# A small store in a two-layer hybrid trunk: the final n of the mLSTM leaves from a 128x4 tile of its own instead of from a column of a larger tile

## The chip, the core and the metric

One core of a Trainium2 chip runs the whole program in one launch. The metric is the device time in microseconds (us), the median of several runs. Names used below: PE is TensorE, with its weight loads beside it; DVE is VectorE; ACT is ScalarE; POOL is GpSimd; SP is SyncE, which here issues almost all DMAs. HBM is the chip's main memory, SBUF the core's own.

## The reference, cut to what matters

Two decoder layers run on 256 prompt positions and 8 single-token samples, 264 columns together. In each layer one input projection feeds three groups of heads (sliding-window attention, a Mamba-2 scan, an mLSTM); an output projection and a squared-ReLU MLP follow. The outputs are the two hidden states and every final state. The part that matters here is the mLSTM over the prompt, in two chunks of 128 positions, for 4 heads of 128 dimensions:

```
C = C * g_end[..., None, None] + einsum('bhk,bkhd,bkhe->bhde', wk, kc, vc)
n = n * g_end[..., None]       + einsum('bhk,bkhd->bhd', wk, kc)
return ..., C, n, m_new        # final C (4,128,128), final n (4,128), per layer
```

The final n of the prompt is an output called n_p: per layer 128 rows of 4 numbers (one per head), 2 KB in all. The kernel gets n with C in one matmul, since the values carry a column of ones behind their 128 columns; C is then 128 columns wide and n is column 128.

## The kernel before, in words

All weights come from HBM in float32 and are used as two parts. A step loads half a weight block, 128 x 1024 numbers (512 KB), into a tile `raw` (3 buffers). ACT casts it into `hi`, DVE subtracts and leaves the rest in `lo`, and PE runs 24 matmuls of 264 columns on it: `acc<-uh,hi` and `acc<-ul,hi` eight times each, then `acc<-uh,lo` eight times. Two such halves make one output block, and 43 blocks make the input projection of a layer.

The work of the three head groups is laid between these matmuls. Nothing is executed in the order in which the source is written: each operation is recorded first (line 196), and `issue` (line 267) simulates the engines with estimated costs and due times and writes each engine's list. All instructions then come from line 410, so the profile puts them all on that line, and they are told apart by tile names. A DMA gets the same cost whatever the size of its pieces: 0.4 us on its queue and its bytes over a fixed rate (line 248). The lists are fixed. An engine that waits for one instruction holds back all that follow it on that engine. Loads of weights and stores of results share SP's one list, and their transfers share the same DMA engines.

The mLSTM is in `mlstm()` (line 1075). Names that the profile shows there: `lB` is a large buffer, whose part `Co` (line 1083) has 4 heads of 130 columns, C in columns 0 to 127 and n in column 128; `hB` holds the weighted keys and the values; `eA` takes the exponentials and squares of ACT; `mw` is a tile of small numbers per row for the normaliser; `srow` holds rows of q and k for the samples. Lines 1132 and 1133 store C_p (128 rows x 4 heads x 512 bytes) and n_p, each by one DMA on SP. The second reads column 128 of `Co`, whose heads are 130 numbers apart, so each of its 512 pieces is one number of 4 bytes. Behind it lie the loop over the two chunks (line 1138) and the mLSTM of the samples (line 1190).

Of the kernel before, what the change touches and what calls it, by code (L numbers as in the profile page):

```python
# [18 lines left out]
P = 128  # L19
# [409 lines left out]
def trunk(ctx, tc, I, O):  # L429
    nc = tc.nc  # L430
    pr = Program(tc)
    vec, act, pool, pe, sync = pr.vec, pr.act, pr.pool, pr.pe, pr.sync
# [8 lines left out]
    def st(shape, tag, dt=F32, bufs=1):  # L441
        return pr.tile(sp, shape, dt, tag, bufs)
# [118 lines left out]
    def mixers(l):  # L561
# [500 lines left out]
        def m_evac(i):  # L1062
            def f(acc):
                if i == 0:
                    t_["m3"] = st((P, 12, T), "m3")
                dst = t_["m3"][:, i]
                if i < 4:
                    stt(out=dst, in0=acc, scalar=KSC, in1=rb, op0=MUL, op1=MUL)
                else:
                    tt(out=dst, in0=acc, in1=rb, op=MUL)  # L1070
                if i == 11:
                    mlstm()
            return f

        def mlstm():
# [7 lines left out]
            Co = MD[:, 520:1040].rearrange("p (h e) -> p h e", h=4)  # L1083
# [46 lines left out]
                for h in range(2):  # L1130
                    stt(out=Co[:, h0 + h, 0:129], in0=C0[:, h0 + h, 0:129], scalar=EG[:, h0 + h, 151:152], in1=cp_[:, h, 0:129], op0=MUL, op1=ADD)
            sync.dma_start(out=O["C_p"][l], in_=Co[:, :, 0:P])
            sync.dma_start(out=O["n_p"][l], in_=Co[:, :, 128])
            qg = st((P, 4, P), "Qm")
            ptt(out=qg, in0=mq[:, :, P:256], in1=EG[:, :, 24:152], op=MUL)

# [394 lines left out]
```

## Time and profile before

| what | value |
|---|---|
| median of 3 runs | 2375.81 us (2373.26 to 2376.09) |
| the profiled execution's own time | 2372.86 us |
| its span, first to last instruction | 2371.1 us |
| PE busy in the span | 2324.2 us (98%) |
| DVE, ACT, POOL busy | 1483.0, 1173.6, 60.6 us |
| mean granted TensorE clock | 0.994 |
| DMA moved | 432.27 MB, mean 182 GB/s |

The profiled execution took 1.8 us more than its span, for what lies around the instructions. A share of busy time is an average over the program; what a change is worth is read from the few microseconds around it. A timeline row gives start, duration, engine, operation, out<-in by tile names, shape and count, and in brackets the idle time before it with what ended it. SPq is the issuing of a DMA, not its transfer. Rows of one kind that follow each other are merged, so "x4" with a long duration spans the waits between the four.

### The profile page before, as it was taken

What the parts mean: (1) busy time and instruction counts of PE and PEld (TensorE: products, weight loads), DVE (VectorE), ACT (ScalarE), POOL (GpSimd) and SP (SyncE); (2) the same over time, 40 slices, a digit from 0 to 9 for tenths busy, and PEclk for the clock granted to TensorE, in tenths of its full rate; (3) what the DMA queues carried; (4) which work ended last, traced back from release to release, by engine and by line L of the source; (5) the groups of instructions that cost most, each with busy time, mean ns of one, the idle gap of its engine ahead of it and who ended that gap; (6) DMA issues with size and microseconds to landing.
All of it is one profiled execution on the core that took longest, in us unless ns stands there. A gap on an engine that the chain in (4) does not pass through costs nothing.

```text
span 2371.1 us, 46293 instructions
## 1 busy us (share of the span) xinstructions
PE 2324.2 (98%) x18874; PEld 2306.8 (97%) x18874; DVE 1483.0 (63%) x2450; ACT 1173.6 (49%) x1979; POOL 60.6 (3%) x138
## 2 busy tenths in 40 slices
PE   8999799999999999999999999999999999999997
PEld 7999799999999999999999998999999999999997
DVE  8789796754554454455686898866545545544555
ACT  5657564543453344354545577455434434434553
POOL 0120000000000000000001100000000000000000
PEclk9999999999999999999999999999999999999999
DMA  7356666555655565565563577555556556655654
GB/s 249 109 181 219 178 213 180 182 180 180 181 182 179 180 184 179 181 183 179 179 201 120 160 249 215 183 182 181 180 180 183 179 179 183 181 179 182 183 178 135
DMA packets 124052, 432.27 MB, mean 182 GB/s; under 512 B 15808, under 2 KB 19264, under 8 KB 123840
## 3 DMA queue, kind: packets, MB, share of 16 engines
q1 hardware_dynamic: 123264, 428.10, 58.9%
q8 instruction: 149, 2.44, 0.4%
q10 hardware_dynamic: 576, 1.22, 0.1%
q14 instruction: 63, 0.52, 0.1%
HBM read 410.10 MB, written 19.16 MB: 181 GB/s over the span
## 4 chain that ended last, share of the span: by engine, by line
PE 91%; DVE 4%; DMA 3%; ACT 1%; issue 1%; SPq 0%; DVEq 0%; ACTq 0%
PE acc L410 86%; PE ms L410 4%; DMA raw<-in_w_in 2%; DVE lo L410 1%; PE sg L410 1%; DMA S<-in_ssm 1%; DMA out_ssm_s<-S 1%; DVE S L410 0%; DVE ac L410 0%; ACT hi L410 0%; DVE m L410 0%; DVE tb L410 0%; DVE xt L410 0%; SPq L410 0%; ACT eA L410 0%
## 5 line engine op out<-in xcount | busy, mean ns | idle before, releaser
L410 ACT CAST hi<-raw 128x1024 fp32r<-128x1024 f32 (+1 forms) x751 | 783.4, 1044 | 979.4 <-PE acc L410 924.1
L410 DVE TENSOR_TENSOR lo<-raw,hi 128x1024 fp32r<-128x1024 f32 (+1 forms) x751 | 912.0, 1215 | 343.6 <-ACT hi L410 336.8
L410 PE MATMUL acc<-uh,hi 128*128 128x264 f32 x3392 | 856.0, 287 | 11.4 <-ACT hi L410 9.0
L410 PE MATMUL acc<-ul,hi 128*128 128x264 f32 x3392 | 847.9, 285 | 0.0
L410 PEld LDWEIGHTS acc<-uh,hi 128*128 128x128 f32 x3392 | 640.8, 189 | 14.6 <-ACT hi L410 10.6
L410 PEld LDWEIGHTS acc<-ul,hi 128*128 128x128 f32 x3392 | 641.2, 189 | 3.6 <-issue 1.4
L410 PE MATMUL acc<-uh,lo 128*128 128x264 f32 x3392 | 484.9, 285 | 0.0
L410 PEld LDWEIGHTS acc<-uh,lo 128*128 128x128 f32 x3392 | 443.3, 189 | 0.6 <-issue 0.5
L410 PE MATMUL acc<-lB,hi 128*128 128x264 f32 x1280 | 320.4, 286 | 0.0
L410 PE MATMUL acc<-hB,hi 128*128 128x264 f32 x1280 | 320.3, 284 | 0.0
L410 PE MATMUL acc<-hA,hi 128*128 128x264 f32 x1280 | 320.2, 285 | 0.0
L410 PE MATMUL acc<-lA,hi 128*128 128x264 f32 x1280 | 319.4, 285 | 0.0
L410 DVE TENSOR_TENSOR xt<-acc,xt 128x264 f32<-128x264 f32 x192 | 83.0, 432 | 264.0 <-PE acc L410 264.0
L410 PEld LDWEIGHTS acc<-hB,hi 128*128 128x128 f32 x1280 | 241.5, 189 | 0.0
L410 PEld LDWEIGHTS acc<-lB,hi 128*128 128x128 f32 x1280 | 241.3, 189 | 0.0
L410 PEld LDWEIGHTS acc<-hA,hi 128*128 128x128 f32 x1280 | 241.1, 188 | 0.0
L410 PEld LDWEIGHTS acc<-lA,hi 128*128 128x128 f32 x1280 | 241.1, 188 | 0.0
L410 PE MATMUL acc<-hB,lo 128*128 128x264 f32 x1280 | 180.9, 284 | 0.0
L410 PE MATMUL acc<-hA,lo 128*128 128x264 f32 x1280 | 180.6, 284 | 0.0
L410 DVE SCALAR_TENSOR_TENSOR ra<-acc,rb 128x264 f32<-128x264 f32 x128 | 55.4, 432 | 197.0 <-PE acc L410 197.0
L410 PEld LDWEIGHTS acc<-hB,lo 128*128 128x128 f32 x1280 | 165.9, 188 | 0.0
L410 PEld LDWEIGHTS acc<-hA,lo 128*128 128x128 f32 x1280 | 164.4, 188 | 0.0
(305 smaller groups left out, 1374.9 us busy)
## 6 DMA issues: line engine op xcount, KB each, us to landing
raw<-in_w_up SPq DMA_DIRECT2D x256, 512.0 KB, 3.6
raw<-in_w_down SPq DMA_DIRECT2D x256, 512.0 KB, 3.6
raw<-in_w_in SPq DMA_DIRECT2D x171, 512.0 KB, 4.2
raw<-in_w_out SPq DMA_DIRECT2D x64, 512.0 KB, 3.6
S<-in_ssm SPq DMA_DIRECT2D x16, 512.0 KB, 5.4
out_ssm_s<-S SPq DMA_DIRECT2D x16, 512.0 KB, 3.6
S<-in_mC SPq DMA_DIRECT2D x8, 512.0 KB, 5.5
out_C_s<-S SPq DMA_DIRECT2D x8, 512.0 KB, 5.1
```

The source lines that it names most:

```text
L410: getattr(eng, method)(*[real(a) for a in args], **{k: real(a) for k, a in kw.items()})
```

## The change

In each of the two layers, ACT copies column 128 of `Co` (4 numbers per row, 130 apart) into a new tile `np`, 128 rows of 4 numbers side by side. The DMA to n_p then reads this tile: 128 pieces of 16 bytes. No other line differs.

```
-            sync.dma_start(out=O["n_p"][l], in_=Co[:, :, 128])
+            np_out = st((P, 4), "np")
+            act.copy(out=np_out, in_=Co[:, :, 128])
+            sync.dma_start(out=O["n_p"][l], in_=np_out)
```

The lists of PE, DVE and POOL stay the same row by row. ACT's list gains one row in each layer. The piece of ACT's list around it in the first layer, where `eA<-sg,qc` are the four exponentials of the first chunk and the cast `hi<-raw` behind them is that of the next weight half (+ marks what is new):

```order
 L410 CAST hi<-raw 128x1024 x3
 L410 ACTIVATE eA<-sg,qc 128x128 x4
+L410 COPY np<-lB 128x4
 L410 CAST hi<-raw 128x1024
 L410 ACTIVATE eA,mw<-ms 128x128 x4
```

The copy stands between the exponentials and that cast; nothing else moved on ACT. The second place is SP's list around the store of n_p, in the first layer too (the second layer's reads the same, but for the names of buffers):

```order
 L410 DMA out_C_p<-lB 512x1x128
-L410 DMA out_n_p<-lB 512x1x1
-L410 DMA raw<-in_w_in 128x1024 x4
+L410 DMA raw<-in_w_in 128x1024
+L410 DMA out_n_p<-np 128x4
+L410 DMA raw<-in_w_in 128x1024 x3
 L410 DMA n0s<-in_mn 128x32
 L410 DMA raw<-in_w_in 128x1024
```

The store of n_p moved behind the first of the four weight loads that followed it, and it now waits for the copy on ACT.

## Rows read from the trace of the kernel before

**Rows 1.** The page: span, busy time and share of PE and its weight loads.

```profile
span 2371.1 us, 46293 instructions
...
PE 2324.2 (98%) x18874; PEld 2306.8 (97%) x18874; DVE 1483.0 (63%) x2450; ACT 1173.6 (49%) x1979; POOL 60.6 (3%) x138
```

**Rows 2.** PE's waits, whole span: releaser, total us, times, longest us.

```profile
PE sg L410 <- ACT eA L410: 14.6, 2, 10.0
```

**Rows 3.** Timeline of PE, first layer.

```profile
249.47 0.39 PE L410 MATMUL sg<-maskb,identb 128*128 128x512 bf16 x1 [1.87 <-DVE S L410]
...
261.28 1.14 PE L410 MATMUL acc<-uh,lo 128*128 128x264 f32 x8
272.38 0.79 PE L410 MATMUL sg<-srow,ssel 128*128 128x512 f32 x1 [9.95 <-ACT eA L410]
```

**Rows 4.** Timeline of ACT, first layer.

```profile
253.61 1.11 ACT L410 ACTIVATE eA<-sg,qc 128x128 f32<-128x128 f32 x4
267.89 1.04 ACT L410 CAST hi<-raw 128x1024 fp32r<-128x1024 f32 x1 [13.16 <-DMA raw<-in_w_in]
...
271.18 1.15 ACT L410 ACTIVATE eA<-sg,qc 128x128 f32<-128x128 f32 x4
272.17 1.08 ACT L410 CAST hi<-raw 128x1024 fp32r<-128x1024 f32 x1
```

**Rows 5.** Timeline of SP's issues, first layer.

```profile
252.07 1.53 SPq L410 DMA_DIRECT2D out_C_p<-lB  x1
253.65 0.63 SPq L410 DMA_DIRECT2D out_n_p<-lB  x1
254.38 16.16 SPq L410 DMA_DIRECT2D raw<-in_w_in  x4
```

**Rows 6.** Chain that ended last, first layer: start, us, what.

```profile
254.38 13.41 DMA raw<-in_w_in
```

**Rows 7.** Windows: us, busy per engine (instructions), PEclk, DMA share, GB/s.

```profile
250.00:255.00 5.00, 5.00 (x44) 5.00 (x43) 5.00 (x14) 4.72 (x10) 1.26 (x1) 1.00 0.67 254
256.00:265.00 9.00, 6.17 (x50) 5.75 (x49) 2.24 (x5) 0.00 (x0) 1.39 (x2) 1.00 0.57 22
1429.00:1433.00 4.00, 4.00 (x36) 4.00 (x35) 1.83 (x5) 0.00 (x0) 0.67 (x1) 1.00 0.77 42
45.50:48.50 3.00, 3.00 (x27) 3.00 (x27) 2.82 (x6) 1.48 (x2) 0.00 (x0) 1.00 1.03 329
262.40:272.40 10.00, 0.05 (x2) 0.02 (x1) 2.66 (x11) 3.30 (x14) 0.00 (x0) 0.66 0.74 166
272.40:275.80 3.40, 3.40 (x12) 2.86 (x13) 3.19 (x11) 1.28 (x2) 0.00 (x0) 0.50 0.24 88
1439.90:1443.10 3.20, 3.19 (x11) 2.65 (x12) 2.99 (x10) 1.32 (x2) 0.00 (x0) 0.50 0.23 83
```

**Rows 8.** Timeline of SP's issues, first layer: small stores ahead of three loads.

```profile
43.30 0.55 SPq L410 DMA_DIRECT2D out_k_p<-tb  x1
43.90 0.57 SPq L410 DMA_DIRECT2D out_v_new<-vnew  x1
```

**Rows 9.** Tile raw: the three loads issued from 45.8 to 52.0 us.

```profile
DMA to landing us min/median/max: 4.9/5.0/5.1
```

**Rows 10.** Timeline of SP, second layer.

```profile
1425.30 0.67 SPq L410 DMA_DIRECT2D out_n_p<-lB  x1
1426.07 12.01 SPq L410 DMA_DIRECT2D raw<-in_w_in  x4
```

**Rows 11.** Timeline of ACT, second layer.

```profile
1426.21 1.11 ACT L410 ACTIVATE eA<-sg,qc 128x128 f32<-128x128 f32 x4
```

**Rows 12.** Second layer: timeline of PE.

```profile
1439.91 0.80 PE L410 MATMUL sg<-srow,ssel 128*128 128x512 f32 x1 [4.66 <-ACT eA L410]
```

**Rows 13.** Second layer: the chain that ended last.

```profile
1426.07 9.26 DMA raw<-in_w_in
```

**Rows 14.** ACT's groups by form: count, busy us, mean ns, idle before.

```profile
L410 ACT COPY dec<-ms 128x16 f32<-128x16 f32 x2 | 0.3, 172 | 0.1
```

## The prediction

> **What bounds the kernel now.** The page comes first: PE is busy for 98% of the span [rows 1], so only a wait of PE, or a slower PE, can be won back. The list of PE's waits comes next. Its largest entry is one pair: `sg` waits for ACT's `eA`, twice, 14.6 us together, 10.0 the longer [rows 2]. The timelines place the pair: 9.95 us before 272.38 in the first layer [rows 3] and 4.66 us before 1439.91 in the second [rows 12], each soon after the store of n_p.
>
> Going back along the first: PE's `sg<-srow` needs the second four exponentials on ACT, which start at 271.18. They stand in ACT's list behind the cast of one weight half, and that cast began at 267.89 after ACT had stood idle for 13.16 us waiting for the load [rows 4]. So PE waits although its own weights are not what it lacks; a cast ahead in ACT's list is late. The load is the first on SP behind the store of n_p [rows 5], issued at 254.38 and 13.41 us under way [rows 6]. The second layer has the same chain with 9.26 us [rows 13].
>
> What are the DMA engines doing meanwhile? The windows tell: 254 GB/s from 250 to 255, then 22 GB/s from 256 to 265 with a busy share of 0.57, and in the second layer 42 GB/s at 0.77 [rows 7]. They are occupied and move nearly nothing, just after 512 pieces of 4 bytes were sent. The check is another small store: v_new (128 pieces of 32 bytes; the code gives the shape), issued at 43.90 beside k_p with its pieces of 512 bytes [rows 8]. The window behind them, 45.5 to 48.5, moves 329 GB/s [rows 7], and the loads issued from then on land in 4.9 to 5.1 us [rows 9]. So pieces of 32 and 512 bytes leave no such hole. I take the 4-byte pieces as its cause; C_p, which stands just ahead of them both times, is the other suspect.
>
> **Part by part.** (1) *The pieces.* The trace has no store of 16-byte pieces. Nearest on one side is v_new with as many pieces, 128, and no hole: cost 0. On the other side is n_p itself: the hole of about 9 us stays (4 in the second layer). Below nothing there is no room, since v_new's window already runs fast. I take 0, because number of pieces and size both stand nearer to v_new (32 bytes, 128) than to 4 bytes, 512.
>
> The Trainium skill's page "DMA: Bandwidth & Descriptors", section Specifications, speaks against this: a transfer of under 512 bytes goes by read-modify-write, and 16 bytes are as far under that line as 4. By that rule n_p stays in the slow class, and the hole may stay too. But v_new is in the class by the same rule, and its window ran at 329 GB/s, so here the trace doesn't bear the class out as the cause of the hole. What the rule would give is rival A.
>
> (2) *The first load moves ahead of the store.* It is issued in n_p's place: 253.65 instead of 254.38, 1425.30 instead of 1426.07 [rows 5, 10]. It is the one load that PE's wait hangs on, and even if n_p stayed slow it would now be in front of it.
>
> (3) *When PE goes on.* The load takes 5.0 us as in rows 9, so it lands at 258.65. In the trace 272.38 − (254.38 + 13.41) = 4.59 us pass from landing to PE's `sg` [rows 3, 6]: cast, squares, exponentials. I leave that as it is: 263.24. PE's earlier work ends at 272.38 − 9.95 = 262.43, so 0.8 us of wait remain, and 9.95 − 0.8 = 9.1 go. Second layer: 1425.30 + 5.0 + 4.59 = 1434.89, before PE's work ends at 1439.91 − 4.66 = 1435.25: all 4.66 go. With a load of 6.9 us, 1.9 us more would stay in the first layer and 1.5 in the second; with 4 us, 0.8 more would go.
>
> (4) *The clock.* After both waits the granted clock is 0.50 for 3.4 us and 3.2 us (1.2 instead of 2.4 GHz), while PE is fully busy; during the long wait it had fallen to a mean of 0.66 [rows 7]. After the shorter wait of 1.87 us that ends at 249.47 [rows 3], the window from 250 to 255 has 1.00 [rows 7]. So with a wait of 0.8 us or none I take the slow stretches as gone: half of 3.4 and of 3.2, 1.7 + 1.6 = 3.3 us. If they stay: 0.
>
> (5) *The copy on ACT.* Two of them, about 0.17 us each, by the copy of 16 numbers per row [rows 14]. Each stands between the exponentials and the cast that waits for the load, where ACT was idle for 13.16 us; with that idle time cut to about 4 us it still costs nothing. Without this cover it would be 0.17 on PE's chain, twice.
>
> (6) *The wait on SP.* n_p now waits for that copy: the exponentials end at 254.72 and 1427.32 [rows 4, 11], so it goes at about 254.9 and 1427.5. SP is free for it at about 254.3 and 1426.0 and stands for 0.6 and 1.5 us. Behind it are three weight loads, the load of n0s and the loads of the samples' C. The second weight load then goes after 0.6 us more, at 255.5 and 1428.1, and lands 5.0 later at 260.5 and 1433.1. Its cast comes 272.17 − 267.89 = 4.28 us after the first cast [rows 4], which by (3) is at 263.0 and 1434.7. It is early by 2.5 and 1.6 us, so this wait costs nothing; beyond these two margins it costs its length.
>
> The sum is 9.1 + 4.66 + 3.3 = 17.1 us (0.7%). The profiled execution took 2372.86 us (1.8 above its span), so it would come to 2355.8. It lies 2.95 below the median shown, and I put the gain to the median: 2375.81 − 17.1 = 2358.7 us. The half of the gain that hangs on the length of the hole is uncertain even in the kernel before, since it was 9 us once and 4 once; that may be what the 2.95 us and the 2.8 us between the runs are made of, and the gain in a median run would then be near 20.
>
> **Rivals.**
>
> *A: 16-byte pieces are as slow as 4-byte ones* (by the rule cited in (1), or because the transfer is still cut into single numbers). For it: nothing in the trace has been seen at 16 bytes. Against it: v_new. The hole keeps its length, but falls on the second load. First layer: it starts 1.25 us later (254.9 against 253.65), so that load lands near 267.8 + 1.25 = 269.0 and is cast by 270.1. PE goes on at 263.2, does the block of 3.4 us at half speed in 1.7, then the first half's 24 matmuls at 1.14/8 us each [rows 3], 3.4: it runs dry at 268.3 and waits 1.8 us, perhaps with a slow stretch of 1.7 behind it. Second layer: the load lands near 1437.5, PE has work until 1440.3, nothing is lost. Gain 17.1 − 1.8 to 3.5 = 13.6 to 15.3, about 2361.5. So the new order on SP alone would bring most of it.
>
> *B: C_p makes the hole.* It stands right ahead of n_p, and its 512 pieces are four to eight times as many as k_p's in rows 8. It is not changed and still goes ahead of the first load; the issue 0.7 us earlier brings nothing while the engines are stuck. 2375.8 us. Against it: k_p's pieces of the same 512 bytes left no hole.
>
> *C: SP's wait turns on PE (slower).* The place is n_p's wait for the copy; the price is its length beyond the margins of (6), for three weight loads and the samples' loads behind it. It decides when the copy comes more than 3 us (0.6 + 2.5) after SP is ready, and it makes the kernel slower only if B holds too, or if it exceeds the 17 us. Under B the second load has the 4.28 us between the casts, so the copy would have to be 5 us late; at 10 us late in both layers: 2375.8 + 2 x 5 = 2386. Against it: everything ahead of the copy on ACT ended 1.1 and 2.0 us after n_p's old issue.
>
> **How the numbers follow.** Forecast 0.76, A 0.12, B 0.09, C 0.03. A measurement of this kernel tells 0.2% (4.8 us) from no change. Forecast and A are faster by more than that, 0.88; B is the same, 0.09; C is slower, 0.03. The forecast's own spread goes from a gain of 22 us (longer holes than in this execution) to 11 (loads of 6.9 us, and slow stretches that stay): 2353.5 to 2365; A lies at 2361.5. The range is 2353 to 2367; what is left out is B, C and the outermost tails.
>
> **What would show it.** The entry `sg` from `eA` of 14.6 us shrinks to about 1 us. The window behind the new n_p runs at over 200 GB/s. The first load behind C_p lands in about 5 us, n_p is issued about 1.3 and 2.2 us later than before, and the second load's cast follows the exponentials without idle time. The clock stays at 1.00 from there on. I am wrong if the hole is there with C_p in front and n_p behind it (B), if it has only moved to the second load (A), or if SP stands long before n_p and ACT waits for the second or third load instead (C).

## The result, and the profile after

The changed kernel takes 2359.74 us (median of 4 runs, 2357.66 to 2361.76); the kernel before, beside it on the same chip, 2375.95 us (4 runs, 2373.26 to 2376.91). That is 16.2 us less, a ratio of 0.9934 with a 95% interval of 0.9916 to 0.9951. The forecast was 2358.7 us, with a range of 2353 to 2367. The profiled executions took 2358.68 and 2372.86 us, 14.2 us apart, and so are their spans.

The page of the changed kernel, to be set against [rows 1]: the span is shorter by 14.2 us, PE's busy time by 2.0 us only. Nearly all that went was waiting.

```profile
span 2356.9 us, 46297 instructions
...
PE 2322.2 (99%) x18874; PEld 2303.6 (98%) x18874; DVE 1483.4 (63%) x2450; ACT 1174.1 (50%) x1981; POOL 61.9 (3%) x138
```

PE's waits in the changed kernel (releaser, total us, times, longest us). The pair of [rows 2] stood at 14.6 us and is now at 1.8; the second line is new, and is told of below.

```profile
PE sg L410 <- ACT eA L410: 1.8, 2, 1.4
...
PE sg L410 <- DVE tb L410: 0.7, 2, 0.5
```

SP's issues in the changed kernel, first layer and then second, where [rows 5, 10] stood. The first load now goes ahead of n_p. SP then stands for about 1.15 us in each layer (254.20 + 0.34 to 255.69, and 1416.21 + 0.34 to 1417.71) until the copy is made.

```profile
252.93 0.60 SPq L410 DMA_DIRECT2D out_C_p<-lB  x1
254.20 0.34 SPq L410 DMA_DIRECT2D raw<-in_w_in  x1
255.69 0.33 SPq L410 DMA_DIRECT2D out_n_p<-np  x1
256.11 6.68 SPq L410 DMA_DIRECT2D raw<-in_w_in  x3
...
1416.21 0.34 SPq L410 DMA_DIRECT2D raw<-in_w_in  x1
1417.71 0.33 SPq L410 DMA_DIRECT2D out_n_p<-np  x1
1418.13 5.74 SPq L410 DMA_DIRECT2D raw<-in_w_in  x3
```

ACT's timeline there, in place of [rows 4]: the copy takes 0.20 us, the cast that had stood idle for 13.16 us now waits 4.47, and the second load's cast, at 264.43, follows the exponentials without idle time.

```profile
255.47 0.20 ACT L410 COPY np<-lB 128x4 f32<-128x4 f32 x1
260.13 1.05 ACT L410 CAST hi<-raw 128x1024 fp32r<-128x1024 f32 x1 [4.47 <-DMA raw<-in_w_in]
...
264.43 1.09 ACT L410 CAST hi<-raw 128x1024 fp32r<-128x1024 f32 x1
```

PE's timeline, both layers: the waits of 9.95 and 4.66 us [rows 3, 12] are 1.39 and 0.46 us.

```profile
264.63 0.50 PE L410 MATMUL sg<-srow,ssel 128*128 128x512 f32 x1 [1.39 <-ACT eA L410]
265.36 0.49 PE L410 MATMUL ms<-hB,eB 128*128 128x129 f32 x2 [0.22 <-DVE eB L410]
...
273.30 1.12 PE L410 MATMUL acc<-uh,lo 128*128 128x264 f32 x8
274.90 1.10 PE L410 MATMUL sg<-srow,ssel 128*128 128x512 f32 x2 [0.48 <-DVE tb L410]
...
1425.71 0.49 PE L410 MATMUL sg<-srow,ssel 128*128 128x512 f32 x1 [0.46 <-ACT eA L410]
...
1434.36 1.13 PE L410 MATMUL acc<-uh,lo 128*128 128x264 f32 x8
```

The chain that ended last, where [rows 6] had the first load at 13.41 us; further on, it now goes by a load of the samples' C.

```profile
254.20 5.83 DMA raw<-in_w_in
...
268.46 5.67 DMA S<-in_mC
```

Two windows, with the columns of [rows 7]: behind the store the DMA engines move 209 GB/s (22 before), and PE's work behind its wait runs at a granted clock of 1.00 (0.50 before).

```profile
256.00:265.00 9.00, 7.36 (x58) 6.72 (x56) 6.07 (x17) 3.65 (x14) 2.23 (x2) 1.00 0.84 209
...
264.60:268.00 3.40, 3.14 (x22) 2.78 (x23) 3.18 (x11) 1.34 (x2) 0.00 (x0) 1.00 0.26 95
```

For the block behind the wait, four more rows of PE's timeline of the kernel before, which answer to those at 265.36, 273.30, 274.90 and 1434.36:

```profile
273.10 0.80 PE L410 MATMUL ms<-hB,eB 128*128 128x129 f32 x2
...
282.26 1.14 PE L410 MATMUL acc<-uh,lo 128*128 128x264 f32 x8
283.24 0.62 PE L410 MATMUL sg<-srow,ssel 128*128 128x512 f32 x2
...
1449.72 1.14 PE L410 MATMUL acc<-uh,lo 128*128 128x264 f32 x8
```

**The account.** First layer: 9.95 − 1.39 = 8.6 us of wait. From `sg<-srow` to the same `acc<-uh,lo` it was 282.26 − 272.38 = 9.88 us and is 273.30 − 264.63 = 8.67, so the clock gives 1.2. Second layer, counted alike: 4.66 − 0.46 = 4.2 us of wait, and (1449.72 − 1439.91) − (1434.36 − 1425.71) = 1.2 of the clock. Together that is about 15.2 us. Some is given back at once: in the kernel before, the next `sg<-srow` followed that `acc` after 0.98 us, and now after 1.60, because PE is early and `tb`, made from the samples' C, is not there yet. Matching the matmuls of the two traces one by one, 1.1 us goes back in this way in the first layer and 0.9 in the second. That leaves 13.2. The remaining 1 us, to 14.2, is the sum of differences of up to 3.1 us and of either sign elsewhere, far from the store. The largest lies near 1387 us of the kernel before: there PE waits 1.78 us for DVE, with 3.3 us at a granted clock of 0.50 behind, and at that place in the changed kernel it waits 0.19 us and the clock stays at 1.00. That these belong to the spread between executions is not shown, but the store stands nowhere near. Between the medians the 14.2 us become 16.2, since 2372.86 us is 3.1 below the median of the kernel before and 2358.68 is 1.1 below that of the changed one.

### The profile page after: what moved, and what is told of

Read it like the earlier page. It is cut to its first block, busy times and chain, and to the rows that moved or that the text cites. A ratio compares the mean times of both kernels' runs of the same rounds, so it can differ in the third digit from the quotient of the medians.

```text
span 2356.9 us, 46297 instructions
## 1 busy us (share of the span) xinstructions
PE 2322.2 (99%) x18874; PEld 2303.6 (98%) x18874; DVE 1483.4 (63%) x2450; ACT 1174.1 (50%) x1981; POOL 61.9 (3%) x138
## 4 chain that ended last, share of the span: by engine, by line
PE 91%; DVE 4%; DMA 3%; ACT 1%; issue 1%; SPq 0%; DVEq 0%; ACTq 0%
PE acc L410 86%; PE ms L410 4%; DVE lo L410 1%; PE sg L410 1%; DMA raw<-in_w_in 1%; DMA S<-in_mC 1%; DVE m L410 1%; DMA out_ssm_s<-S 0%; DMA S<-in_ssm 0%; DVE ac L410 0%; ACT hi L410 0%; DVE tb L410 0%; DVE xt L410 0%; DVE ra L410 0%; DVE S L410 0%
```

## The experiments

Two theories stood at the start. T1: the 512 pieces of 4 bytes make the hole, and 16-byte pieces make none. T2 (rival A): the pieces stay slow, and what helps is that the first load goes ahead of the store. B, that C_p makes the hole, was the third. In the table, "wait" is PE's `sg` from `eA`, first and second layer, and "landing" the time from issue to landing of the first three weight loads issued behind the n_p store in the first layer (behind C_p where there is no n_p), as far as the trace has their landings (two or three of them). Both are of one profiled execution, which need not be like the median one. Ratios are to the kernel before on the same chip, whose median was 2377.83 us beside e1 to e4, 2377.78 beside e5, e6, e9 and a1, and 2376.41 beside the rest; the times of different chips are not to be compared directly.

| run | store of n_p, per layer | time, us | ratio (95%) | wait, us | landing, us |
|---|---|---|---|---|---|
| before | 512 x 4 B, 4 B apart | 2375.95 | 1 | 9.95 / 4.66 | 13.4 to 14.4 |
| changed | 128 x 16 B, behind one load | 2359.74 | 0.9934 (0.9916, 0.9951) | 1.39 / 0.46 | 6.7 to 7.3 |
| e1 | 512 x 4 B, behind one load | 2371.89 | 0.9979 (0.9969, 0.9989) | 6.92 / 4.37 | 14.7 to 15.9 |
| e2 | 128 x 16 B, old order | 2364.23 | 0.9950 (0.9935, 0.9965) | 4.22 / 1.38 | 8.3 to 8.7 |
| e3 | none | 2361.23 | 0.9936 (0.9922, 0.9951) | 1.28 / 0 | 5.6 to 5.7 |
| e4 | as before, no C_p | 2377.38 | 1.0000 (0.9991, 1.0010) | 9.40 / 5.93 | 13.5 to 13.7 |
| e6 | 128 x 4 B, 16 B apart | 2364.59 | 0.9949 (0.9934, 0.9964) | 4.03 / 0.72 | 8.1 to 8.6 |
| e7 | 256 x 8 B, 8 B apart | 2370.12 | 0.9973 (0.9963, 0.9982) | 7.63 / 2.55 | 11.1 to 12.2 |
| e5 | 512 x 4 B, 64 B apart | 2364.19 | 0.9948 (0.9933, 0.9963) | 2.63 / 0 | 6.6 to 7.1 |
| e9 | 512 x 4 B, 512 B apart | 2359.84 | 0.9930 (0.9915, 0.9944) | 2.04 / 1.00 | 5.6 to 6.8 |
| e8 | within C_p's rows | 2360.09 | 0.9933 (0.9921, 0.9946) | 1.48 / 0 | 5.7 to 5.9 |
| e11 | as before, layers exchanged | 2377.48 | 1.0000 (0.9991, 1.0009) | 8.59 / 6.60 | 12.7 to 13.5 |
| a1 | changed, beside e5, e6, e9 | 2361.86 | 0.9937 (0.9920, 0.9953) | 3.12 / 0.72 | 6.9 to 7.5 |
| a2 | changed, beside e7, e8, e11 | 2360.62 | 0.9938 (0.9926, 0.9950) | 2.99 / 0.16 | 6.1 to 6.9 |

**e1_small_pieces_new_order: the copy and the new order, but small pieces.** The tile is two numbers wide per head, so the store still has 512 pieces of 4 bytes.

```
-            np_out = st((P, 4), "np")
-            act.copy(out=np_out, in_=Co[:, :, 128])
-            sync.dma_start(out=O["n_p"][l], in_=np_out)
+            np_out = st((P, 4, 2), "np")
+            act.copy(out=np_out[:, :, 0], in_=Co[:, :, 128])
+            sync.dma_start(out=O["n_p"][l], in_=np_out[:, :, 0])
```

> The tile np is spread to every second number, so that the store of n_p again moves 512 pieces of 4 bytes; the copy on ACT and the order of the changed kernel stay. If the pieces make the hole (my theory), it comes back, but behind the first weight load: the DMA engines move under 60 GB/s for 4 to 9 us after n_p, ACT stands idle before the SECOND load's cast, PE's wait of sg for eA stays near 2 us, and the time is 2359 to 2365 us, between the changed kernel and the kernel before and nearer to the changed one. If the order alone brings the gain (rival), there may be any hole, and the time is that of the changed kernel, 2359.7 us within 2. If C_p makes the hole (rival), nothing changes against the changed kernel and no hole stands behind n_p.

The new order alone gives 0.21% (0.11 to 0.31), about 5 us. Of what was expected only the hole came (32 GB/s in the window below, under 60 expected): the time is above 2359 to 2365 us, and PE's wait is 6.92 us and not near 2, because the hole delayed the first load too. SP's timeline, the chain (second layer last), ACT's timeline and a window of the first layer:

```profile
252.66 0.58 SPq L410 DMA_DIRECT2D raw<-in_w_in  x1
253.80 0.56 SPq L410 DMA_DIRECT2D out_n_p<-np  x1
```

```profile
252.66 11.02 DMA raw<-in_w_in
...
1421.63 9.08 DMA raw<-in_w_in
```

```profile
263.79 1.04 ACT L410 CAST hi<-raw 128x1024 fp32r<-128x1024 f32 x1 [10.01 <-DMA raw<-in_w_in]
```

```profile
260.00:264.00 4.00, 1.35 (x12) 1.15 (x10) 0.00 (x0) 0.21 (x1) 0.00 (x0) 1.00 0.60 32
```

The load was issued 1.14 us ahead of the store and still took 11.02 us: the hole (32 GB/s) catches what is already under way. In the second layer a load issued 1.50 us ahead took 9.08 us. Being ahead in SP's list did not protect a load that was still under way. This refutes rival A as it was priced.

The kernel before shows the same on the store of C_p, which is issued 1.58 us ahead of n_p there. Its landing in the first layer, in the kernel before and then in the kernel without n_p (e3):

```profile
DMA to landing us min/median/max: 9.4/9.4/9.4
...
DMA to landing us min/median/max: 3.7/3.7/3.7
```

**e2_large_pieces_old_order: 16-byte pieces, nothing else.** The store reads the last C columns and n of head 3, four numbers side by side, so other numbers go out as n_p; it stays in its old place, without the copy.

```
-            sync.dma_start(out=O["n_p"][l], in_=Co[:, :, 128])
+            sync.dma_start(out=O["n_p"][l], in_=Co[:, 3, 125:129])
```

> The kernel before, but n_p is stored as 128 pieces of 16 bytes straight from Co (columns 125 to 128 of head 3 instead of column 128 of the four heads, so the values of n_p are others); no copy, the store stays ahead of all four weight loads. If the pieces make the hole, it is gone: over 200 GB/s behind n_p, first load landing in 5 to 7 us, wait of sg for eA under 4 us, time 2358 to 2362 us. If the order brought the gain, the time stays at 2374 to 2377 us with a wait near 14 us.

The landing of the three loads behind the store, and PE's timeline:

```profile
DMA to landing us min/median/max: 8.3/8.6/8.7
```

```profile
267.88 0.49 PE L410 MATMUL sg<-srow,ssel 128*128 128x512 f32 x1 [4.22 <-ACT eA L410]
```

The larger pieces alone give 0.50% (0.35 to 0.65), some 12 us, most of the gain. But they are not free, and here too the expectation failed: in the first layer the first loads took 8.3 to 8.7 us (5 to 7 expected), about 3 us more than behind no n_p (next), 5.6 us of PE's wait stay over both layers (under 4 expected), and the time is above 2358 to 2362 us.

**e3_no_n_p and e4_no_C_p: which store makes the hole.**

```
-            sync.dma_start(out=O["n_p"][l], in_=Co[:, :, 128])      (e3)
-            sync.dma_start(out=O["C_p"][l], in_=Co[:, :, 0:P])      (e4)
```

> The kernel before without the store of n_p (that output is left unwritten). The floor for this place. If n_p's pieces make the hole, it is gone, and the time is 2357 to 2361 us, at most 3 us under the changed kernel, since 16-byte pieces cost nearly nothing. If C_p makes the hole, the time stays at 2374 to 2377 us.

> The kernel before without the store of C_p (that output is left unwritten); n_p goes out in 512 pieces of 4 bytes. If n_p makes the hole, it stays: wait of sg for eA 8 to 15 us, time 2368 to 2376 us (the first load is free of C_p's 256 KB, some 1 us a layer). If C_p makes it, the wait falls under 4 us and the time to 2358 to 2361 us.

Landing without n_p:

```profile
DMA to landing us min/median/max: 5.6/5.6/5.7
```

Landing without C_p:

```profile
DMA to landing us min/median/max: 13.5/13.6/13.7
```

The hole goes with n_p and stays without C_p: rival B is refuted. Leaving C_p out gave nothing that can be measured (1.0000), where 1 us a layer was expected. e3 is also the floor: with no store at all the kernel is not measurably faster than the changed one (0.9936 against 0.9934 to 0.9938), though its chain keeps 1.28 us of wait in the first layer.

**e6_128_pieces_of_4B and e7_256_pieces_of_8B: size or number.** e6 stores n of one head only, 128 pieces of 4 bytes, 16 bytes apart. e7 stores columns 127 and 128 of heads 2 and 3, 256 pieces of 8 bytes.

```
+            sync.dma_start(out=O["n_p"][l, :, 0:1], in_=Co[:, 3, 128:129])                              (e6)
+            sync.dma_start(out=O["n_p"][l].rearrange("p (a b) -> p a b", b=2), in_=Co[:, 2:4, 127:129])  (e7)
```

> The kernel before, but n_p stores only one head: 128 pieces of 4 bytes, 16 bytes apart in HBM (the other three heads' n is left out), ahead of the four loads. Theory 'number of pieces': the hole is that of 128 pieces of 16 bytes in the same place (measured wait 5.6 us, ratio 0.995): wait 4 to 7 us, ratio 0.994 to 0.9965. Theory 'size': a piece of 4 bytes costs more than one of 16, the wait is 8 us or more, ratio above 0.997.

> The kernel before, but n_p is stored as 256 pieces of 8 bytes from Co (columns 127 and 128 of heads 2 and 3, so other values), ahead of the four loads. If the hole grows with the number of small pieces into the same 2 KB, it lies between 128 pieces (first loads landing in 8.1 to 8.7 us in the first layer) and 512 pieces (13.4 to 14.4): about 10 to 10.5 us; wait of sg for eA 7 to 10 us; ratio 0.9955 to 0.998. If only 4-byte pieces are slow, it is as with 128 pieces, 0.995.

Landing in e6:

```profile
DMA to landing us min/median/max: 8.1/8.5/8.6
```

Landing in e7:

```profile
DMA to landing us min/median/max: 11.1/11.9/12.2
```

128 pieces cost the same at 4 bytes (8.1 to 8.6 us) as at 16 (8.3 to 8.7). In the same 2 KB of HBM, 128, 256 and 512 pieces give some 8.5, 12 and 14 us; for 256, 10 to 10.5 was expected. Between 4 and 16 bytes, it is not the size of a piece that counts here.

**e5_spread_64B and e9_spread_512B: the same 512 pieces, spread out.** The output tensor gets room, so that each 4-byte piece lands 64 or 512 bytes from the next.

```
-            sync.dma_start(out=O["n_p"][l], in_=Co[:, :, 128])
+            sync.dma_start(out=O["n_p"][l, :, :, 0], in_=Co[:, :, 128])
...
-            n_p=(L, P, 4)
+            n_p=(L, P, 4, 16)     (e5; 128 in place of 16 in e9)
```

> The kernel before (512 pieces of 4 bytes, ahead of the four loads), but in HBM the numbers of n_p lie 64 bytes apart instead of side by side (the output is 16 times as wide, and the first of each 16 is taken). Theory 'number of pieces': nothing changes, wait of sg for eA 12 to 16 us, ratio to the kernel before 0.999 to 1.001. Theory 'neighbours': the hole comes from many small writes into the same few bytes of HBM; then it shrinks to under a third, wait under 5 us, ratio 0.993 to 0.996.

> As the 64-byte spread, but 512 bytes apart in HBM, so that the 512 numbers are spread over 256 KB as C_p's rows are. Theory 'number of pieces': wait of sg for eA 12 to 16 us, ratio 0.999 to 1.001, as in the kernel before. Theory 'neighbours': wait under 3 us, ratio 0.993 to 0.9945, below the 64-byte spread if what collides is wider than 64 bytes, and equal to it if not.

Landing at 64 bytes:

```profile
DMA to landing us min/median/max: 6.6/7.0/7.1
```

Landing at 512 bytes:

```profile
DMA to landing us min/median/max: 5.6/6.5/6.8
```

Still 512 pieces of 4 bytes, in the old order, without the copy. At 512 bytes apart the kernel gains as much as by the change, 0.9930 against 0.9937 on the same chip; at 64 bytes it gains 0.52% (0.37 to 0.67), about as much as with 128 pieces (e6). So the number alone doesn't do it either. Nor is it the reading side: the store reads the same 512 numbers out of `Co` as in the kernel before, and only where they are written differs. What the runs fit is how closely the pieces lie in HBM: in the first layer 4, 8, 16, 64 and 512 bytes apart give some 14, 12, 8.5, 7 and 6.5 us. In the second layer it is 9.2 to 9.3, 6.8 to 7.0, 5.1 to 5.9, 4.8 to 5.7 and 5.3 to 6.0, with 3.7 to 5.5 behind no n_p: there 16, 64 and 512 bytes can't be told apart. At 4 to 16 bytes the number falls as the distance grows, so the two are apart only in e5 and e9; a count of pieces per stretch of HBM would fit as well as the distance from one to the next.

**e8_n_with_C: no small store at all.** C and n of a row leave as one piece of 2064 bytes.

```
-            Co = MD[:, 520:1040].rearrange("p (h e) -> p h e", h=4)
+            Co = MD[:, 520:1036].rearrange("p (h e) -> p h e", h=4)
...
-            sync.dma_start(out=O["C_p"][l], in_=Co[:, :, 0:P])
-            sync.dma_start(out=O["n_p"][l], in_=Co[:, :, 128])
+            sync.dma_start(out=O["Cn_p"][l], in_=Co)
```

> A version to beat both: Co is made 129 columns wide, so that C and n of a row lie side by side, and one DMA stores both, 128 pieces of 2064 bytes, into one output of 4 x 129 per row, which is taken apart afterwards; no store of n_p, no copy. By the theory 'neighbours' there is no hole: first loads landing in 5 to 6 us, wait of sg for eA under 3 us, ratio to the kernel before 0.992 to 0.9945, equal to or up to 3 us below the changed kernel beside it. If the pieces of 512 bytes of C_p cost anything by themselves, it is under the kernel without n_p (0.9936).

Landing behind the joint store:

```profile
DMA to landing us min/median/max: 5.7/5.8/5.9
```

PE's timeline:

```profile
267.07 0.49 PE L410 MATMUL sg<-srow,ssel 128*128 128x512 f32 x1 [1.48 <-ACT eA L410]
```

2360.09 against 2360.62 us for the changed kernel on the same chip: no difference that can be measured, with one DMA less per layer and no copy. No version tried beats the changed kernel by more than the intervals tell apart. The nearest to it is e9, whose four runs (2359.36 to 2361.07 us) all lie under the four of a1 (2361.30 to 2363.83).

**e11_layers_swapped: why the second hole is shorter.** Each layer stores into the other's part of n_p.

```
+            sync.dma_start(out=O["n_p"][1 - l], in_=Co[:, :, 128])
```

> The kernel before, but the two layers' n_p go into each other's half of the output (put back afterwards). The first layer's hole has been longer than the second's in every run. If the address sets the length, it is the second layer's that is longer now (wait of sg 4 to 6 us in the first layer, 8 to 10 in the second). If the place in the program sets it (what else is in flight), the first layer's stays longer (8 to 10 us against 4 to 6). Time as the kernel before in either case, ratio 0.999 to 1.001.

PE's waits in the two layers:

```profile
272.60 0.79 PE L410 MATMUL sg<-srow,ssel 128*128 128x512 f32 x1 [8.59 <-ACT eA L410]
...
1444.24 0.80 PE L410 MATMUL sg<-srow,ssel 128*128 128x512 f32 x1 [6.60 <-ACT eA L410]
```

The first layer keeps the longer wait, so the address doesn't decide it alone. But the second went from 4.66 to 6.60 us, and e4 has 5.93 there with no address changed. One execution of each can't tell such a shift from the spread between runs, so this stays open.

**a1_changed_again and a2_changed_beside** are the changed kernel itself, beside the others on their chips.

> The changed kernel, on the same chip as the runs beside it, for a ratio that can be set against theirs: 0.9925 to 0.9945 (first measured as 0.9934), wait of sg for eA 1 to 3 us.

> The changed kernel on the chip of the merged store, for their comparison: 0.9925 to 0.9945.

The ratio repeats (0.9937, 0.9938). The first layer's wait does not: 1.39, 3.12 and 2.99 us in three profiled executions. In the last two the first load, the one that goes ahead of the store, took 7.20 and 7.43 us instead of 5.83, and the granted clock behind the wait was 0.50 and 0.55 instead of 1.00. The chain, PE's timeline and the window behind the wait, in a1 and then in a2:

```profile
253.76 7.20 DMA raw<-in_w_in
265.56 0.79 PE L410 MATMUL sg<-srow,ssel 128*128 128x512 f32 x1 [3.12 <-ACT eA L410]
265.50:268.90 3.40, 3.34 (x12) 2.81 (x13) 3.15 (x11) 1.37 (x3) 0.00 (x0) 0.50 0.27 95
...
254.31 7.43 DMA raw<-in_w_in
266.33 0.53 PE L410 MATMUL sg<-srow,ssel 128*128 128x512 f32 x1 [2.99 <-ACT eA L410]
266.30:269.70 3.40, 3.17 (x12) 2.73 (x13) 3.18 (x11) 1.34 (x2) 0.00 (x0) 0.55 0.27 94
```

These two executions took 2363.83 and 2364.11 us, 2.0 and 3.5 above the medians of a1 and a2, while the 2358.68 us of the first is 1.1 below its median. So a median run would lie between what the three traces show.

## Why the prediction came out right, and where its steps failed

The time was right, and so was the main mechanism: n_p's pieces made the hole (e3, e4), PE's wait hung on the one load behind them, and most of the wait went: 14.6 us over both layers became 1.8, 3.8 and 3.1 in the three profiled executions. Steps (1) to (4) were wrong in part, on different sides.

**Step (1), the pieces at 0, failed.** 16-byte pieces do delay loads behind them: 8.3 to 8.7 us against 5.6 to 5.7 with no n_p in the first layer (e2, e3). I had leant on v_new, with 128 pieces of 32 bytes and no hole behind it. By the runs, the distance in HBM matters, and v_new's pieces lie twice as far apart as those of 16 bytes; whether that is why it left no hole was not tried. The rule of the Trainium skill that I weighed there ("DMA: Bandwidth & Descriptors", Specifications) is that under 512 bytes a transfer goes by read-modify-write. The runs agree with it further than I allowed: 16 bytes are indeed not free, and 4 bytes cost the same at the same number (e6, e2). But 512 pieces of 4 bytes, 512 bytes apart, leave a kernel as fast as with no store (e9, 0.9930; e3, 0.9936), and they are under that line too. Size under 512 bytes alone is not the cause.

**Step (2) and rival A, the order, failed.** Both said that a load in front of a slow store is safe; A put the gain of the order alone at 13.6 to 15.3 us. e1 measured about 5, because the load was still under way when the small pieces went out (11.02 us). The pieces alone give 12 us (8 to 15, e2), the order alone 5 (3 to 7, e1), both 16 (12 to 20), as much as leaving the store out (e3): within these intervals the two simply add up.

The two errors lean against each other: the 16-byte pieces still cost something, and going ahead takes a part of that cost off the one load that PE hangs on. How large a part is not settled. That load landed after 5.83 us in the first profiled execution, nearly as with no store (5.73, e3), but after 7.20 and 7.43 us in a1 and a2, and after 8.26 in the old order (e2). That the forecast sums up to the measured time is in this part luck. The loads behind the store land in 6.1 to 7.5 us and not in 5.0. Their casts have cover: the second load's came without idle time in all three executions, as forecast.

**Step (3)** held to a microsecond in the first profiled execution: the load took 5.83 us instead of 5.0, and 1.39 and 0.46 us of wait are left instead of 0.8 and 0. In a1 and a2 the length of the load was wrong by more than 2 us and left 3.12 and 2.99 us, near the 0.8 + 1.9 that the step gives for a load of 6.9 us.

**Step (4), the clock, was mis-sized, and did not hold in every run.** In the first profiled execution both slow stretches went as forecast, but they gave 1.2 + 1.2 = 2.4 us, not 3.3. I had halved the whole stretch. Not all of it is paced by PE: from `sg<-srow` to the next `ms<-hB,eB` it is 0.73 us at the full clock and was 0.72 at half, since that matmul waits for DVE's `eB` (0.22 us, timeline of PE, 265.36). In a1 and a2, behind waits of 3.12 and 2.99 us, the slow stretch of the first layer stayed (0.50 and 0.55); only the second layer's went.

**Steps (5) and (6)** held. The copy took 0.20 us (0.17 forecast). SP stood for about 1.15 us in each layer (0.6 and 1.5 forecast), and the second load's cast was not late for it.

What no step had: about 2 us goes back right behind the old wait, where PE now arrives ahead of the samples' C. With the clock (0.9 less) and the waits that are left (1.0 less), and 1 us more from elsewhere, it makes 14.2 us of the 17.1 for the profiled pair.

What the runs don't show is where in the memory or its path the small pieces block the reads. The trace has the DMA engines occupied and moving little; why closeness costs so much stays open.

## What to carry to other kernels

A store of a few kilobytes can cost ten microseconds, and on a load that has nothing to do with it: look for a window with busy DMA engines and few GB/s, and take the store just ahead of it as the suspect. Make its pieces fewer, or lay them further apart, or let them ride in the rows of a larger store; all three came to the time without the store here, the first together with a load moved ahead, the second at 512 bytes apart (at 64 it gained 12 us). To price such a change, undo each half of it by itself, since two wrong terms can add up to the right time.

## What was not expected of the hardware

With 512 writes of 4 bytes into the same 2 KB ahead of them, loads of 512 KB took 13.4 to 14.4 us in the first layer; with the same 512 writes spread 512 bytes apart, 5.6 to 6.8; with none, 5.6 to 5.7. The hole also reached back to a load issued 1.14 us before the store, which took 11.02 us.
